# Norms in place on VectorE with four tiles in flight, and a later order of the small products in dilated attention

## Chip, core and metric

The kernel runs on one core of a Trainium2 chip. The engines are TensorE (PE), VectorE (DVE), ScalarE (ACT), GpSimd (POOL) and the queue of SyncE (SP), which issues nearly all transfers. The time is the device time of one execution in microseconds (us); lower is better.

## What is computed

The kernel is one layer of an encoder: x is 1024 positions by 1024 channels in float32. Every sub-layer stands between two RMS norms, and the attention is a mixer of two branches.

```python
h = x + 0.5 * post1(SwiGLU_1(pre1(x)))
h = h + postm(Mixer(prem(h)))
h = h + 0.5 * post2(SwiGLU_2(pre2(h)))

def rms_norm(x, g):
    xf = x.astype(jnp.float32)
    y = xf * lax.rsqrt(jnp.mean(xf * xf, axis=-1, keepdims=True) + EPS)
    return (y * g.astype(jnp.float32)).astype(x.dtype)
...
for pm, ps, pn in parts:          # dilated attention: maximum, denominator, numerator of each pattern
    wgt = jnp.exp(pm - m_all)
    num = wgt * pn if num is None else num + wgt * pn
    den = wgt * ps if den is None else den + wgt * ps
return (num / den).astype(q.dtype)
```

The mixer projects its input once, runs a dense latent attention and the dilated attention (8 heads of 64 channels), projects each by a branch matrix, weighs them by sigmoid gates, adds them, and ends with an output projection.

## The kernel before

The 1024 positions are eight tiles of 128. Every float32 product is made of three products of halves (`xh`, `xl`, `wh`, `wl`: a value rounded, and the rest).

**Who sets the order.** At build time a planner (class `Plan`) runs all parts as processes on a model of the engines. A process asks for an engine with a modelled cost (`act(700, ex)` is a cost of 700 columns), a queue per engine serves the lowest rank first, and `Event` and `Tokens` hold processes back. The order in which the queues are served becomes each engine's instruction order on the chip. So a changed cost, or a `yield 1.0` (a pause in the model), makes no instruction longer; it only moves instructions in the queues. Each engine then works strictly in its order.

**Norms.** `postnorm` takes the result `y` of a sub-layer (in the FFN the accumulator `acc`, filled by L1171; in the mixer `y`, filled by L2560). ACT squares it (L501), POOL makes `rstd` (L309, L311), the gain `y*g` is written to a tile `xn` of its own by POOL for the first 512, 384 or more columns and by DVE for the rest (both L490), and DVE makes `res = xn*rstd + res` (L514). `prenorm` squares `res` (L443), scales it with `rstd` and its gain on DVE (L453), in two of the three places with the last 256 columns by ACT and POOL (L459, L460), and hands the tile to `put`. `put` transposes it on TensorE (L428), ACT casts the result to `xh` (L432) and DVE takes the rest as `xl` (L433). In the second FFN `put` also makes differences of tiles (`xt`, L416). `norm_tok = Tokens(2)` lets two tiles into this chain at a time.

**Dilated attention.** For each head DVE takes the scores from TensorE with their maxima (L2138), ACT takes exponentials (L2149), and two small products with a selection matrix bring the numbers of the patterns together: DVE makes `z` (L2160), TensorE the first product (L2169), a chain of short DVE and ACT steps follows (L2176 to L2205), then `z` again (L2210), the second product (L2217) and `a` (L2228). Then DVE weighs the exponentials (L2246), TensorE transposes them, ACT and DVE split them to `ptd` (L432, L433), and TensorE makes the product with the values. DVE adds its halves to `oT` and `tb` (L2315, L2320), POOL adds the two (L2322), and the result is stored (`ob_d`, L2323). Between these steps TensorE has matmuls of the gate projection (L1495) as filler, and when they are gone those of `branch_a` (L2444). When the last head is stored, `take` loads the heads' results in four pieces (L2378), ACT and POOL split them, and the products of `branch_b` begin; the merge makes `mt` from them (L2521 to L2525) and the output projection follows.

## Time and profile before

| | |
|---|---|
| median of 3 runs | 2434.36 us (2431.82 to 2435.98) |
| profiled execution, device time | 2432.88 us |
| its span in the profile | 2430.7 us |
| TensorE busy | 2294.6 us, 94% of the span |
| VectorE, ScalarE, GpSimd busy | 66%, 43%, 32% |
| granted clock of TensorE, mean | 0.974 of full speed |

The span runs from the first to the last instruction; 2.2 us of the device time lie around it. A busy share is an average over stages: an engine that is busy a third of the whole time may be the one that is waited for in one stage. The granted clock is 1 at 2.4 GHz and 0.5 at 1.2 GHz.

### The profile page before, as it was taken

The numbers are of one execution on the slowest core, as the hardware profiler recorded it, in microseconds if no ns is written. First come the engines' busy times: TensorE is split into PE (matmuls) and PEld (weight loads), VectorE is DVE, ScalarE is ACT, GpSimd is POOL, SyncE is SP. The second block draws the span as 40 slices with busy tenths as digits, with TensorE's granted clock in tenths as the row PEclk, the third lists the DMA queues.
The fourth block names the chain that finished last, engine by engine and source line by source line (L and its number), as shares of the span: only waits on it lengthen the run. The fifth ranks groups of instructions, "written<-read, shape, count | busy, mean of one in ns | idle before, by whom it ended". The sixth has DMA issues, their size and how long they took to land. (4 is left out here: it accounts for less than half of the span.)

```text
span 2430.7 us, 30689 instructions
## 1 busy us (share of the span) xinstructions
PE 2294.6 (94%) x11096; PEld 1920.7 (79%) x11096; DVE 1609.8 (66%) x2669; ACT 1044.0 (43%) x1952; POOL 784.1 (32%) x592
## 2 busy tenths in 40 slices
PE   6999999999979999999998898988979999999997
PEld 4788888788869987888886777776868888887885
DVE  7877878875672105666666766347787778778658
ACT  6233434431153336666655545454433334344111
POOL 2000000354274555756532322575300000006443
PEclk9999999999989999999999999999979999999998
DMA  6234434587352133122223222675533444357762
GB/s 186 83 130 139 173 127 163 195 321 254 134 173 70 62 98 100 38 72 65 61 82 90 79 73 85 194 258 180 182 108 113 163 140 173 116 197 280 259 238 104
DMA packets 197145, 350.17 MB, mean 144 GB/s; under 512 B 32577, under 2 KB 112961, under 8 KB 196481
## 3 DMA queue, kind: packets, MB, share of 16 engines
q1 hardware_dynamic: 196992, 348.21, 42.6%
q8 instruction: 87, 1.43, 0.2%
q14 instruction: 66, 0.53, 0.1%
HBM read 234.78 MB, written 113.38 MB: 143 GB/s over the span
## 5 line engine op out<-in xcount | busy, mean ns | idle before, releaser
L706 PE MATMUL s<-xh,wt 128*128 128x512 f32 x1408 | 453.8, 393 | 10.2 <-DVE uu L807 9.0
L524 POOL TENSOR_TENSOR wdb<-rawd,wdb 128x1024 fp32r<-128x1024 f32 x34 | 87.3, 2567 | 892.4 <-ACT wdb L523 889.3
L706 PE MATMUL b<-xh,wt 128*128 128x512 f32 x1056 | 345.7, 394 | 0.7 <-ACT xh L432 0.6
L706 PEld LDWEIGHTS s<-xh,wt 128*128 128x128 f32 x1408 | 266.2, 189 | 69.8 <-DVE uu L807 10.7
L706 PE MATMUL s<-xl,wt 128*128 128x512 f32 x704 | 275.7, 392 | 0.0
L706 PEld LDWEIGHTS b<-xh,wt 128*128 128x128 f32 x1056 | 200.9, 190 | 44.0 <-ACT xh L432 1.0
L706 PE MATMUL b<-xl,wt 128*128 128x512 f32 x528 | 207.7, 393 | 0.9 <-DVE xl L433 0.9
L1134 PE MATMUL b<-wdb,ha 128*128 128x512 f32 x864 | 202.5, 389 | 0.0
L1134 PE MATMUL s<-wdb,ha 128*128 128x512 f32 x816 | 190.5, 389 | 0.0
L1134 PEld LDWEIGHTS b<-wdb,ha 128*128 128x128 f32 x864 | 162.4, 188 | 33.8
L1134 PEld LDWEIGHTS s<-wdb,ha 128*128 128x128 f32 x816 | 153.1, 188 | 31.8
L1495 PE MATMUL b<-xh,wh 128*128 128x512 f32 x384 | 162.7, 424 | 1.4 <-DVE o L2016 0.8
L1966 POOL TENSOR_TENSOR p<-p,rd 128x1024 f32<-128x1024 f32 x64 | 122.5, 1923 | 117.7 <-DVE rd L1963 112.5
L706 PEld LDWEIGHTS s<-xl,wt 128*128 128x128 f32 x704 | 133.3, 189 | 27.4
L1495 PE MATMUL b<-xl,wh 128*128 128x512 f32 x384 | 153.2, 399 | 0.0
L675 ACT CAST wt<-s 128x512 fp32r<-128x512 f32 x176 | 104.2, 617 | 113.9 <-DVE s L635 59.0
L1495 PE MATMUL b<-xh,wl 128*128 128x512 f32 x384 | 152.9, 398 | 0.0
L524 POOL TENSOR_TENSOR wdb<-td,wdb 128x1024 fp32r<-128x1024 f32 x40 | 108.1, 2706 | 109.7 <-ACT wdb L523 98.6
L428 PE MATMUL b<-cst,p 128*128 128x128 f32 x768 | 107.2, 280 | 22.2 <-DVE ptd L433 14.9
L524 POOL TENSOR_TENSOR wl<-raw,wh 128x512 fp32r<-128x512 f32 (+3 forms) x88 | 110.0, 1267 | 53.5 <-ACT wh L523 46.5
L428 PEld LDWEIGHTS b<-cst,p 128*128 128x128 f32 x768 | 90.1, 143 | 40.0 <-DVE ptd L433 17.5
L676 DVE TENSOR_TENSOR wt<-s,wt 128x512 fp32r<-128x512 f32 x176 | 117.9, 684 | 5.4 <-ACT wt L675 5.1
(298 smaller groups left out, 4989.8 us busy)
## 6 DMA issues: line engine op xcount, KB each, us to landing
hs_d<-hl SPq DMA_DIRECT2D x112, 512.0 KB
ha<-hs_d SPq DMA_DIRECT2D x56, 1024.0 KB
raw<-in_ffn_w_gate_dram SPq DMA_DIRECT2D x48, 512.0 KB
raw<-in_ffn_w_up_dram SPq DMA_DIRECT2D x48, 512.0 KB
rawd<-in_ffn_w_down_dram SPq DMA_DIRECT2D x44, 512.0 KB
raw<-in_w_in_dram SPq DMA_DIRECT2D x28, 512.0 KB
h<-res SPq DMA_DIRECT2D x16, 512.0 KB
lg_d<-lg SPq DMA_DIRECT2D x32, 256.0 KB
```

The source lines that it names most:

```text
L428: T.transpose(b[:rows, i * P : (i + 1) * P], src(i), ident)
L524: yield pool(n, lambda: G.tensor_sub(lo, src, hi))
L675: yield act(512, lambda: A.copy(w[:, 0], src))
L676: yield dve(512, lambda: V.tensor_sub(w[:, 1], src, w[:, 0]))
L706: T.matmul(out(), l, r, start=(first and k == 0 and n == 0), stop=(k == 3 and n == 2), skip_group_check=True,)
L1134: T.matmul(ps, l, r, start=(fresh and n == 0), stop=(n == 5), skip_group_check=True)
L1495: T.matmul(bs.ps, l, r, start=(part == 0 and n == 0), stop=(part == 7 and n == 2))
L1966: yield pool(S, lambda: G.tensor_tensor(bx.p, bx.p, bx.rd.broadcast_to([P, S]), op=ALU.mult))
```

## The change

In the norms the gain is multiplied into `y` itself, all 1024 columns at once and by DVE alone, behind ACT's square; the following `prenorm` writes into the same tile, in two halves on DVE alone, and four tiles are let in. In `put`, two of the four differences are written over the old tile. In the dilated attention the modelled costs of the exponential, of the two steps between the small products and of the weighing are raised, and a pause stands ahead of each small product.

```diff
@@ -105,13 +105,12 @@
     return c
 
 
-PRE1, PREM, PRE2 = 768, 768, D
-POOL1, POOLM, POOL2 = [512] * 8, [384] * 8, [512] * 4 + [1024, 768, 512, 512]
 GATES_FROM = 4
 
 AT_BUFFERS = 7712
 HELD = 4
 EARLY = 4
+NORM = 4
 W0 = 4
 
 
@@ -410,8 +409,8 @@
                     old = [ob[0][:, 0:512], ob[0][:, 512:1024]]
                 for ev in (*scaled, *olds):
                     yield ev
-                tt = [slot([P, 2, 512], name="xt") for _ in range(2)]
-                t1, t2, t3, t4 = tt[0][:, 0, :], tt[0][:, 1, :], tt[1][:, 0, :], tt[1][:, 1, :]
+                tt = slot([P, 2, 512], name="xt")
+                t1, t2, t3, t4 = old[0], tt[:, 0, :], tt[:, 1, :], old[1]
                 for i, o, a_, b_ in ((4, t1, xs[0], old[0]), (5, t2, xs[1], t1), (6, t3, xs[1], xs[0]), (3, t4, old[1], t2)):
                     yield dve(512, lambda: V.tensor_sub(o, a_, b_))
                     spawn(self.block(i, j, o), rank)
@@ -433,7 +432,7 @@
         yield dve(n * P, lambda: V.tensor_sub(lo, box[0], hi))
         plan.release(B1)
 
-    def prenorm(src, g, X, t, rank, split_at, xn=None):
+    def prenorm(src, g, X, t, rank, xn=None):
 
         bx, rs = [], []
 
@@ -446,31 +445,22 @@
         yield act(D + 100, sq)
         yield from rstd_steps(bx[1], D, rs)
         xn = bx[0]
-        m = split_at
-        scaled = [Event(), Event((m > 512) + (m < D))]
-
-        def on_dve(c0, c1, ev):
+        scaled = [Event(), Event()]
+
+        def scale(c0, c1, ev):
             yield dve(c1 - c0, lambda: V.scalar_tensor_tensor(
                 xn[:, c0:c1], src[:, c0:c1], rs[0], g()[:, c0:c1], op0=ALU.mult, op1=ALU.mult,
             ))
             plan.set(ev)
 
-        def on_pool(c0, c1, ev):
-            yield act(c1 - c0, lambda: A.mul(xn[:, c0:c1], src[:, c0:c1], rs[0]))
-            yield pool(c1 - c0, lambda: G.tensor_mul(xn[:, c0:c1], xn[:, c0:c1], g()[:, c0:c1]))
-            plan.set(ev)
-
-        spawn(on_dve(0, 512, scaled[0]), rank)
-        if m > 512:
-            spawn(on_dve(512, m, scaled[1]), rank)
-        if m < D:
-            spawn(on_pool(m, D, scaled[1]), rank)
+        for n in range(2):
+            spawn(scale(512 * n, 512 * n + 512, scaled[n]), rank)
         yield from X.put(t, xn, scaled, rank)
 
     def store(dst, src, kb):
         yield dma(kb, lambda: load(dst, src))
 
-    def postnorm(y, g, res_src, dst, t, box, junk, pool_cols, parts=1):
+    def postnorm(y, g, res_src, dst, t, box, junk, parts=1):
 
         bx, rs = [], []
 
@@ -481,37 +471,26 @@
 
         yield dma(512, ld)
         res = box[0]
-
-        m = pool_cols(t)
-        gained = Event((m > 0) + (m < D))
-
-        def gain_of(cols, eng):
-            def write():
-                eng.tensor_mul(xn[:, cols], y[:, cols], g()[:, cols])
-
-            n = cols.stop - cols.start
-            yield (pool if eng is G else dve)(n, write)
-            plan.set(gained)
-
-        xn = slot([P, D], name="xn")
-        box.append(xn)
+        box.append(y)
+        gained = Event()
 
         def sq():
             ssq = small([P, 1], name="ssq")
             A.activation(junk(), y, AF.Square, accum_out=ssq)
             bx.append(ssq)
 
-        if m:
-            spawn(gain_of(slice(0, m), G), 0)
-        if m < D:
-            spawn(gain_of(slice(m, D), V), 8)
+        def gain_of():
+            yield dve(D, lambda: V.tensor_mul(y, y, g()))
+            plan.set(gained)
+
         yield act(D + 100, sq)
+        spawn(gain_of(), 2)
         yield from rstd_steps(bx[0], D, rs)
         yield gained
         n = D // parts
         for q in range(parts):
             cs = slice(n * q, n * q + n)
-            yield dve(n, lambda: V.scalar_tensor_tensor(res[:, cs], xn[:, cs], rs[0], res[:, cs], op0=ALU.mult, op1=ALU.add))
+            yield dve(n, lambda: V.scalar_tensor_tensor(res[:, cs], y[:, cs], rs[0], res[:, cs], op0=ALU.mult, op1=ALU.add))
             spawn(store(dst[t * P : (t + 1) * P, cs], res[:, cs], 512 // parts), 6)
 
     def raw_tile(w, r0, nk, c0, n):
@@ -1232,7 +1211,7 @@
 
             yield dma(512, ld)
             yield gains0
-            yield from prenorm(bx[0], lambda: gb["g1"], X1, t, 3, PRE1)
+            yield from prenorm(bx[0], lambda: gb["g1"], X1, t, 3)
 
         spawn(one(0), 0)
         yield 0.01
@@ -1245,7 +1224,7 @@
 
     spawn(begin(), 0)
     tail1 = Event()
-    norm_tok = Tokens(2)
+    norm_tok = Tokens(NORM)
 
     def post1(y, t):
         if t == 0:
@@ -1256,8 +1235,8 @@
         yield gains1
         yield norm_tok
         bx = []
-        yield from postnorm(y, lambda: gb["p1"], a["x"], h1, t, bx, lambda: gb["j1"], POOL1.__getitem__)
-        yield from prenorm(bx[0], lambda: gb["gm"], Xm, t, 3, PREM, bx[1])
+        yield from postnorm(y, lambda: gb["p1"], a["x"], h1, t, bx, lambda: gb["j1"])
+        yield from prenorm(bx[0], lambda: gb["gm"], Xm, t, 3, bx[1])
         plan.release(norm_tok)
 
 
@@ -2148,7 +2127,7 @@
                     w = hb.p[i][n // 4][:, n % 4, :]
                     A.activation(w, w, AF.Exp, bias=negm[:, i, n : n + 1], accum_out=md[:, i, 1, n : n + 1])
 
-            yield act(700, ex)
+            yield act(1100, ex)
             plan.set(mev[i])
 
         for i in (1, 0):
@@ -2161,6 +2140,7 @@
             z, md[:, 1].rearrange("p i n -> p (i n)")[:, None, :].broadcast_to([P, 4, 16]),
             mj[:, :, None].broadcast_to([P, 4, 16]), op=ALU.mult,
         ))
+        yield 1.0
         yield B1
         bx = Box()
 
@@ -2192,8 +2172,8 @@
             V.tensor_sub(ee[:, 0, :], md[:, 0, 0, :], mall)
             V.tensor_sub(ju(ee[:, 1, :]), zz[:, :, 0, :], ju(mall))
 
-        yield dve(300, comb)
-        yield act(16, lambda: A.activation(ee, ee, AF.Exp))
+        yield dve(500, comb)
+        yield act(250, lambda: A.activation(ee, ee, AF.Exp))
         wden = small([P, 2, 8], name="wden", bufs=2)
         rd = small([P, 8], name="rdall", bufs=2)
 
@@ -2204,12 +2184,13 @@
             V.reciprocal(rd, rd)
             V.tensor_mul(ee, ee, rd[:, None, :].broadcast_to([P, 2, 8]))
 
-        yield dve(500, comb2)
+        yield dve(900, comb2)
         plan.set(ev[0])
         z2 = small([P, 4, 8], name="z2", bufs=2)
         yield dve(32, lambda: V.tensor_tensor(
             z2, ee[:, 1, None, :].broadcast_to([P, 4, 8]), mm4[:, :, None].broadcast_to([P, 4, 8]), op=ALU.mult,
         ))
+        yield 2.0
         yield B1
 
         def ex2():
@@ -2245,7 +2226,7 @@
                     f = hb.ee[:, 0, n : n + 1] if i == 0 else hb.a23[:, n : n + 1]
                     V.tensor_scalar(w, w, f, None, op0=ALU.mult)
 
-            yield dve2(512 + 100, wgt)
+            yield dve2(512 + 350, wgt)
 
             def block(n):
                 if i == 1:
@@ -2565,8 +2546,8 @@
             yield ev
             yield norm_tok
             bx = []
-            yield from postnorm(y, lambda: gb["pm"], h1, h2, t, bx, lambda: gb["jm"], POOLM.__getitem__)
-            yield from prenorm(bx[0], lambda: gb["g2"], X2, t, 3, PRE2, bx[1])
+            yield from postnorm(y, lambda: gb["pm"], h1, h2, t, bx, lambda: gb["jm"])
+            yield from prenorm(bx[0], lambda: gb["g2"], X2, t, 3, bx[1])
             plan.release(norm_tok)
 
         def outproj():
@@ -2623,7 +2604,7 @@
             gb["j2"] = half_slot([P, D], mybir.dt.bfloat16, name="junk")
             plan.set(gains2)
         yield gains2
-        yield from postnorm(y, lambda: gb["p2"], h2, out, t, [], lambda: gb["j2"], POOL2.__getitem__, 2 if t == NT - 1 else 1)
+        yield from postnorm(y, lambda: gb["p2"], h2, out, t, [], lambda: gb["j2"], 2 if t == NT - 1 else 1)
 
     def second():
         yield out_started
```

TensorE has the same instructions as before, in the same order in both FFNs and in the latent attention. POOL has 38 instructions fewer. The lines of the changed file are some 20 lower: L490 is L483 there, L514 is L493, L453 is L451, L1171 is L1150, L2160 is L2139, L2320 is L2301, L524 is L503.

VectorE where the first FFN ends and the mixer begins, before (each `acc` and `xn` is one tile of 128 positions, `res` its residual, `b` a result of TensorE):

```order
L490 TENSOR_TENSOR xn_5168<-acc_3847,p_738_5058 128x512
L1171 TENSOR_TENSOR acc_3857<-acc_3857,b_5076 128x512
L514 SCALAR_TENSOR_TENSOR res_5132<-xn_5168,rstd_5187,res_5132 128x1024
L1171 TENSOR_TENSOR acc_3870<-acc_3870,b_5085 128x512
L453 SCALAR_TENSOR_TENSOR xn_5144<-res_5122,rstd_5210,gm_5093 128x512
L1171 TENSOR_TENSOR acc_3870<-acc_3870,b_5095 128x512
L453 SCALAR_TENSOR_TENSOR xn_5144<-res_5122,rstd_5210,gm_5093 128x256
L1171 TENSOR_TENSOR acc_3881<-acc_3881,b_5103 128x512
L453 SCALAR_TENSOR_TENSOR xn_5168<-res_5132,rstd_5237,gm_5093 128x512
L1171 TENSOR_TENSOR acc_3881<-acc_3881,b_5113 128x512
L453 SCALAR_TENSOR_TENSOR xn_5168<-res_5132,rstd_5237,gm_5093 128x256
```

And the same stretch now; `acc_3818` to `acc_3850` are the first four tiles:

```order
L483 TENSOR_TENSOR acc_3850<-acc_3850,p_734_5038 128x1024
L1150 TENSOR_TENSOR acc_3870<-acc_3870,b_5114 128x512
L493 SCALAR_TENSOR_TENSOR res_5122<-acc_3837,rstd_5177,res_5122 128x1024
L1150 TENSOR_TENSOR acc_3880<-acc_3880,b_5124 128x512
L1150 TENSOR_TENSOR acc_3880<-acc_3880,b_5136 128x512
L493 SCALAR_TENSOR_TENSOR res_5134<-acc_3850,rstd_5189,res_5134 128x1024
L1150 TENSOR_TENSOR acc_3889<-acc_3889,b_5152 128x512
L1150 TENSOR_TENSOR acc_3889<-acc_3889,b_5167 128x512
L451 SCALAR_TENSOR_TENSOR acc_3818<-res_5102,rstd_5198,gm_5073 128x512 x2
L451 SCALAR_TENSOR_TENSOR acc_3827<-res_5112,rstd_5222,gm_5073 128x512 x2
L451 SCALAR_TENSOR_TENSOR acc_3837<-res_5122,rstd_5229,gm_5073 128x512 x2
L432 TENSOR_TENSOR xl_5235<-b_5237,xh_5233 128x4x128
```

Two tiles were normed and handed on (L453) ahead of the evacuations of the later ones. Now the evacuations of all eight (L1150) come first, and four tiles are scaled one behind the other (L451, two halves each), with no instruction of POOL among them.

VectorE in the third head, before, where `z` for the first small product stands behind `tb`, from which POOL adds `oT`:

```order
L2138 ISA md_11435 128x1
L2320 TENSOR_TENSOR tb_11566<-s_11541,tb_11566 64x1024
L2138 ISA p_1952_11437,md_11435<-b_11582,b_1742_10296 128x256
L2138 ISA md_11435 128x1
L2160 TENSOR_TENSOR z_11597<-md_11435,cst 128x64
L2138 ISA p_1952_11437,md_11435<-b_11575,b_1742_10296 128x256
```

And now:

```order
L2117 ISA md_11384 128x1
L2139 TENSOR_TENSOR z_11580<-md_11384,cst 128x64
L2117 ISA p_1941_11386,md_11384<-b_11560,b_1730_10244 128x256
L2117 ISA md_11384 128x1
L2301 TENSOR_TENSOR tb_11559<-s_11534,tb_11559 64x1024
L2117 ISA p_1941_11386,md_11384<-b_11568,b_1730_10244 128x256
L2117 ISA md_11384 128x1
```

`z` now stands ahead of `tb`. Of the seven heads 2 to 8, `z` stood behind `tb` in all seven; now it stands ahead in heads 3, 5 and 7, and behind in 2, 4, 6 and 8. On TensorE, 9 to 12 filler matmuls and mostly 21 in all stood between the two small products, and now 30 to 39 in most heads; ahead of the first there were 15 to 18 and there are 12 to 21. All in all a head uses about 24 fillers more, so that the gate projection is used up a head earlier.

POOL behind the last head, before (`ro` is a piece of the heads' results, `wl` and `wo` parts of weights):

```order
L2322 TENSOR_TENSOR oT_13500<-oT_13500,tb_13673 64x1024
L524 TENSOR_TENSOR wl_13738<-raw_13713,wh_13737 128x1024
L524 TENSOR_TENSOR xl_13286<-ro_13746,xh_13284 128x1024
L524 TENSOR_TENSOR wl_13782<-raw_13758,wh_13781 128x4x128 x2
L524 TENSOR_TENSOR wl_13820<-raw_13794,wh_13819 128x1024
L524 TENSOR_TENSOR xl_13286<-ro_13807,xh_13284 128x1024
```

And now:

```order
L2303 TENSOR_TENSOR oT_13600<-oT_13600,tb_13781 64x1024
L503 TENSOR_TENSOR wo_13874<-rawo_13865,wo_13874 128x1024
L503 TENSOR_TENSOR wl_13870<-raw_13858,wh_13869 128x4x128 x2
L503 TENSOR_TENSOR xl_12859<-ro_13867,xh_12857 128x1024
L503 TENSOR_TENSOR wo_13885<-rawo_13880,wo_13885 128x1024
L503 TENSOR_TENSOR xl_12859<-ro_13886,xh_12857 128x1024
L503 TENSOR_TENSOR wo_13895<-rawo_13891,wo_13895 128x1024
```

A split of `wo` and one of `wl` now stand between the last `oT` and the first `xl`, and one of `wo` between the first and the second. On TensorE, 117 matmuls of `branch_a` stood between the last head's last product and the first product of `branch_b`; now 57 do. The first twelve matmuls behind these need the first piece, the next the second.

## Rows read from the trace of the kernel before

**Rows 1.** Busy time and granted clock by stretch (columns in the first line)

```profile
core 0: us, PE busy (x) PEld busy (x) DVE busy (x) ACT busy (x) POOL busy (x), PEclk, DMA share, GB/s
...
660.00:760.00 100.00, 82.97 (x487) 75.17 (x487) 70.18 (x83) 44.62 (x91) 63.75 (x70) 0.93 0.39 129
...
1240.00:1545.00 305.00, 269.71 (x1373) 226.01 (x1372) 210.74 (x600) 160.09 (x398) 89.84 (x53) 0.94 0.29 83
...
1590.00:1725.00 135.00, 118.25 (x496) 94.98 (x495) 88.80 (x100) 71.36 (x115) 84.05 (x58) 0.94 0.64 219
...
1750.00:1810.00 60.00, 46.35 (x205) 36.37 (x204) 52.46 (x80) 28.51 (x51) 13.68 (x16) 0.77 0.42 145
...
2390.00:2431.00 41.00, 24.32 (x104) 18.84 (x102) 33.98 (x38) 9.21 (x16) 24.01 (x24) 0.84 0.41 154
```

**Rows 2.** TensorE's waits in the dilated attention: us in total, times, longest

```profile
PE b L428 <- DVE ptd L433: 14.9, 7, 4.4
...
PE b L2169 <- DVE z L2160: 8.5, 4, 3.0
...
PE b L2217 <- DVE z L2210: 4.6, 6, 1.8
...
PE b L428 <- DVE a L2228: 4.0, 2, 2.0
```

**Rows 3.** TensorE's waits from the first FFN to the mixer

```profile
PE b L285 <- DVE xl L433: 6.8, 3, 3.2
...
PE b L285 <- DVE acc L1171: 3.7, 1, 3.7
```

**Rows 4.** VectorE's groups there: count, busy, mean ns, idle before

```profile
L453 DVE SCALAR_TENSOR_TENSOR xn<-res,rstd,gm 128x512 f32<-128x512 f32 (+1 forms) x16 | 20.0, 1281 | 4.5 <-POOL rstd L311 4.5
...
L514 DVE SCALAR_TENSOR_TENSOR res<-xn,rstd,res 128x1024 f32<-128x1024 f32 x8 | 14.8, 1852 | 6.5 <-POOL xn L490 5.1 <-POOL rstd L311 1.4
...
L490 DVE TENSOR_TENSOR xn<-acc,p 128x512 f32<-128x512 f32 x8 | 5.4, 700 | 0.1
```

**Rows 5.** TensorE's waits in merge and output projection

```profile
PE b L428 <- DVE ga L2521: 5.1, 2, 3.7
...
PE b L285 <- DVE ga L2521: 3.4, 1, 3.4
```

**Rows 6.** Timeline of one head's first small product: start, length, engine, line

```profile
1391.35 2.38 POOL L2322 TENSOR_TENSOR oT<-oT,tb 64x1024 f32<-64x1024 f32 x1
...
1393.69 2.47 POOL L524 TENSOR_TENSOR wl<-raw,wh 128x512 fp32r<-128x512 f32 x2
...
1391.69 4.56 DVE L2160 TENSOR_TENSOR z<-md,cst 128x64 f32<-128x64 f32 x1
```

**Rows 7.** Timeline: the norm's VectorE operations beside no GpSimd multiplication

```profile
1690.05 0.75 DVE L453 SCALAR_TENSOR_TENSOR xn<-res,rstd,g 128x512 f32<-128x512 f32 x1 [0.79 <-POOL rstd L311]
...
2403.45 1.28 DVE L514 SCALAR_TENSOR_TENSOR res<-xn,rstd,res 128x1024 f32<-128x1024 f32 x1 [1.50 <-POOL rstd L311]
```

**Rows 8.** Timeline behind the last head's last product

```profile
1543.62 0.51 PE L285 MATMUL s<-ptd,vv 128*128 128x256 f32 x3
...
1549.45 0.58 SPq L2378 DMA_DIRECT2D ro<-ob_d  x1
...
1556.21 2.41 POOL L524 TENSOR_TENSOR xl<-ro,xh 128x1024 fp32r<-128x1024 f32 x1 [4.94 <-ACT xh L523]
...
1563.82 2.40 POOL L524 TENSOR_TENSOR xl<-ro,xh 128x1024 fp32r<-128x1024 f32 x1 [0.33 <-ACT xh L523]
```

**Rows 9.** Timeline: products 128x512 one behind the other

```profile
1742.11 11.04 PE L285 MATMUL b<-wo,mt 128*128 128x512 f32 x48
```

**Rows 10.** VectorE's groups at the end of the program

```profile
L514 DVE SCALAR_TENSOR_TENSOR res<-xn,rstd,res 128x1024 f32<-128x1024 f32 (+1 forms) x9 | 16.0, 1785 | 3.0 <-POOL rstd L311 2.8
...
L1171 DVE TENSOR_TENSOR acc<-acc,b 128x512 f32<-128x512 f32 x16 | 10.6, 677 | 0.1
...
L490 DVE TENSOR_TENSOR xn<-acc,p 128x512 f32<-128x512 f32 (+1 forms) x7 | 5.4, 765 | 0.1
```


## Prediction

> **What bounds the kernel now.** I read the windows first: TensorE's busy time and granted clock, stretch by stretch. In the FFNs and the latent attention TensorE is all but never idle and its order stays as it is, so the change acts only in the stretches of [rows 1]. There the loss of a stretch is its idle time, plus the share of the clock that is missing times its length. From the first FFN to the mixer (660 to 760) that is 100 - 83 = 17.0 us idle and 0.07 x 100 = 7 us of clock, in the dilated attention 35.3 and 18.3, in merge and output projection (1590 to 1725) 16.8 and 8.1, around the second FFN's norm (1750 to 1810) 13.7 and 13.8. In the last stretch TensorE is done early and VectorE, busy for 34.0 of 41 us, sets the end. So a microsecond of idle TensorE comes with about half a microsecond of lost clock (18.3 / 35.3 and 8.1 / 16.8 are both near 0.5; at the mixer 0.4), and I price a removed wait at 1.5 times its length there.
>
> Then I read the waits: which instruction comes last in each stretch. In the dilated attention it is VectorE's `ptd` (14.9 us), the two `z` (8.5 and 4.6) and `a` (4.0) [rows 2]; at the mixer `xl` (6.8) and `acc` (3.7) [rows 3]; in the merge `ga`, twice (5.1 and 3.4) [rows 5]. All of them are VectorE's, and all are short operations. So the third view is the timeline: why is VectorE late? Its `z` of 64 columns takes 4.56 us, from 1391.69 to 1396.25, while GpSimd adds `oT` (2.38) and splits `wl` (2.47), one behind the other, until 1396.16 [rows 6]. VectorE stood still for as long as GpSimd had work. The norm shows the same in its means: `res` of 1024 columns takes 1.28 us when GpSimd has no multiplication and an `L453` of 512 columns 0.75 [rows 7], but in the stretch to the mixer they take 14.8 us for 8 and 20.0 for 16 (half of these are of 256) [rows 4].
>
> The page SBUF — State Buffer of the Trainium skill (section Who interferes with whom) says that a VectorE instruction with two inputs in SBUF and a GpSimd instruction that reads SBUF exclude each other for the whole instruction. This trace agrees: 4.56 us against 2.38 + 2.47.
>
> **First FFN to mixer.** Before, VectorE had 20.0 + 14.8 + 5.4 = 40.2 us of norm here, and 11.0 us of idle time in front of it (6.5 + 4.5) [rows 4]. Now it has 16 halves of 0.75, 8 `res` of 1.28 and 8 gains of 1024, which the trace doesn't show; a gain of 1024 has two inputs like `res`, and I take 1.28 [rows 7]. That is 12.0 + 10.2 + 10.2 = 32.4 us, and the waits for `rstd` (4.5 + 1.4 [rows 4]) stay. VectorE saves 51.2 - 38.3 = 12.9 us. TensorE can get back at most the 10.5 us in which it waited for the norm [rows 3], and not all of it: with four tiles handed on at once it waits in two blocks instead of four. I take half, 5.3, with 0.4 of clock: **-8 us**. Bounds: all 10.5 and its clock, -15; and +4, if a gain of 1024 is as slow as the slow rows (1.85 [rows 4]) and nothing else gets shorter.
>
> **Dilated attention.** With 30 to 39 fillers of 11.04 / 48 = 0.23 us [rows 9] between the two small products, 7 to 9 us, the chain between them is covered; the 4.6 us of the second `z` [rows 2] go. The first `z` was late behind GpSimd's addition, and in heads 3, 5 and 7 it now stands ahead of `tb`, on which that addition waits; I take 5 of the 8.5 us. The waits for `ptd` and `a` I leave: GpSimd still splits weights beside the weighing. 9.6 x 1.5 = **-14 us**. Bounds: with half of `ptd` and `a` gone too, -26; and 0, if each wait only moves to the next step of the same head.
>
> **Behind the last head** the cover is paid for. The last product ends at 1544.1; the first load of the results goes out at 1549.45, and the `xl` of the two pieces end at 1558.6 and 1566.2 [rows 8], 14.5 and 22.1 us behind it. Before, 117 fillers (27 us) hid that. Now 57 fillers last 13.1 us: TensorE waits 1.4 us for the first piece, has 12 products (2.8 us), and waits from 17.3 to 22.1 for the second. That is 6.2 us, with clock **+9 us**. What stands in GpSimd's queue ahead of the first `xl`, a `wo` and a `wl`, fits into the load's time if their weights are there. Bounds: +2, if pieces come as soon as they can (the first load was not waited for before), and +18, if GpSimd's two `wo` (2.4 us each, like the `xl` in [rows 8]) and the stores ahead of the second load in SyncE's queue come on top.
>
> **Merge and output projection.** The `ga` for which TensorE waits, 5.1 + 3.4 us [rows 5], stand behind norm operations that were held by GpSimd's gains. Those gains are gone, and two pairs of products are now made ahead. 8.5 x 1.5 = **-12 us**; bounds -19 (the other waits of the stretch as well) and 0, since four tiles of norm (4 x (1.28 + 1.28 + 1.5) = 16 us by [rows 7]) now stand in one block ahead of a `ga`.
>
> **Second FFN's norm.** The last four tiles no longer wait for one another, but VectorE has all their gains and differences to do in one go and TensorE has fewer fillers left. Going through VectorE's new order with the durations above, the first product that needs all four tiles comes some 2 us earlier relative to the work done, which is less than I can tell: **0 us**, 6 either way. The first norm at the start has 8 x 256 columns more on VectorE (about 3 us by [rows 7]) and 8 short GpSimd steps less: 0, 3 either way.
>
> **End.** VectorE had 16.0 + 10.6 + 5.4 = 32.0 us and waited 3.0 [rows 10]. Now: the same 10.6, 8 gains (10.2), 7 `res` of 1.28 and two halves of 0.75 (10.5): 31.3, and one wait for the last `rstd`, 0.7. **-3 us**; bounds -4 and +3 (gains at 1.85).
>
> The transfers keep their number and size within one instruction, and the exponentials and weighings have their old lengths, since only the planner's costs were raised; what covers them is the same TensorE work.
>
> **Sum:** -8 - 14 + 9 - 12 - 3 = -28 on the profiled execution's 2432.9 us (2430.7 of span and 2.2 around it; the median of the runs shown is 1.5 higher): **2405 us**.
>
> **The rivals.**
> *VectorE becomes the bound (the other side).* The change puts 16,128 columns on it (start 2048, mixer 6144, merge 3072, end 4864): 15.75 x 1.28 = 20 us [rows 7], all in stretches where VectorE is what is waited for. If freeing it from GpSimd gives nothing back, the norms cost 20 us instead of winning 23, and the time is 2432.9 + 20 - 14 + 9 = 2448. It decides from the point where the relief in the norms is under 10 us in all. For it: VectorE is busy for 34 of the last 41 us and GpSimd for 24 [rows 1]. Against it: at the end alone `res` shows 16.0 - 10.5 = 5.5 us of holding and 3.0 of waits [rows 10]. The Trainium skill's page Perfetto Trace Analysis (section Identifying the Most-Contended Engine) says to relieve the engine with the highest occupancy first; here work goes to it, and by that rule this rival would be the outcome.
>
> *The wait moves on.* The heads' chain, not TensorE's order, sets their time; what is no longer waited for at `z` is waited for at `ptd`, which is the largest wait already [rows 2]. The term is 0 instead of -14: 2419. In favour: four heads keep `z` behind `tb`.
>
> *More than I count.* Half of `ptd` and `a` goes too (-26), and all merge waits (-19): 2432.9 - 8 - 26 + 9 - 19 - 3 = 2386.
>
> *No effect.* The gains and the stall behind the last head cancel: 2433.
>
> **How the numbers follow.** Forecast 0.60, VectorE the bound 0.10, the wait moves on 0.17, more than I count 0.08, no effect 0.05. The forecast's own spread, from half of the distance to each term's bounds taken together, is about 2390 to 2422. The 8-in-10 range takes in both middle rivals: 2385 to 2430, leaving VectorE as the bound and no effect outside. 0.2% of 2434 is 4.9 us, about what a measurement of this kernel can tell from no change. Faster by more: the forecast, the moved wait and the larger gain, 0.85 less their slow tails, 0.83. Slower by more: 0.10. Within: 0.07.
>
> **What would show it.** Right: TensorE's waits for the second `z` are gone and those for the first under 4 us; `res` in the norms has a mean near 1.3 us; a new wait of some 5 to 7 us stands behind the last head, before the second half of the first `branch_b` product; between 1590 and 1725 no wait for `ga` over 2 us; in the last stretch VectorE's busy time falls from 34.0 us to about 31 and the waits of `res` for `rstd` from 3.0 to under 1.5. Wrong: `L451` or `L493` wait for `rstd` for more than 10 us in one stretch (GpSimd's small steps held by VectorE's long rows); the waits for `ptd` grow by what `z` lost; or the stall behind the last head is over 12 us, because a `wo` or `wl` whose weights are late holds GpSimd's queue.

## The result and the profile after

The changed kernel takes 2391.85 us (median; 2389.76 to 2394.81) against 2435.17 in the same session: ratio 0.9825, 95% interval 0.9808 to 0.9842. That is 43 us faster where 28 were forecast, inside the range of 2385 to 2430. The time lies 13 us from the forecast of 2405 and 6 us from the rival "more than I count" (2386). The profiled span is 2387.8 us, with a mean granted clock of 0.979.

The windows of the kernel after, cut where its own stages lie (they answer to [rows 1]):

```profile
core 0: us, PE busy (x) PEld busy (x) DVE busy (x) ACT busy (x) POOL busy (x), PEclk, DMA share, GB/s
...
656.00:756.00 100.00, 84.85 (x520) 77.00 (x519) 65.42 (x80) 41.13 (x82) 50.98 (x60) 0.93 0.36 124
1232.00:1524.00 292.00, 277.86 (x1473) 235.83 (x1472) 219.53 (x605) 166.59 (x408) 95.02 (x55) 0.99 0.32 96
1524.00:1562.00 38.00, 28.92 (x113) 21.49 (x111) 5.58 (x5) 18.33 (x25) 28.79 (x15) 0.91 0.86 297
1562.00:1696.00 134.00, 122.89 (x521) 97.62 (x522) 88.33 (x109) 72.31 (x117) 75.28 (x54) 0.95 0.61 210
1696.00:1771.00 75.00, 61.81 (x273) 49.44 (x271) 65.06 (x95) 29.52 (x52) 11.51 (x18) 0.84 0.41 141
2349.00:2388.00 39.00, 24.80 (x110) 20.21 (x108) 33.87 (x42) 9.21 (x16) 11.21 (x16) 0.87 0.27 108
```

In the dilated heads (second row) TensorE is idle for 292.00 - 277.86 = 14.1 us, and the clock takes 0.01 x 292 = 2.9: a loss of 17.1 us, where [rows 1] gave 35.3 + 18.3 = 53.6. Behind the last head (third row) the loss is 9.1 + 3.4 = 12.4, where before only 1.6 was lost. In merge and second norm (fourth and fifth row) it is 17.8 + 25.2 = 43.0, where it was 23.5 + 27.2 = 50.7. Around the first norm (first row) 15.2 us are idle, little less than the 17.0 of before. The rows of before behind the last head, in the merge and in the second norm, cut at the same instructions:

```profile
1543.90:1594.10 50.20, 48.59 (x216) 39.90 (x215) 5.19 (x7) 25.24 (x37) 30.63 (x17) 1.00 0.81 270
1594.10:1733.60 139.50, 124.36 (x523) 100.38 (x524) 93.78 (x108) 72.91 (x117) 84.24 (x59) 0.94 0.61 206
1733.60:1808.60 75.00, 61.35 (x271) 48.84 (x270) 63.51 (x96) 29.14 (x52) 16.42 (x20) 0.82 0.43 146
```

TensorE's waits in the heads (us in total, times, longest), 1232 to 1524, against [rows 2]:

```profile
PE b L427 <- DVE za L2205: 4.2, 5, 1.2
PE b L2198 <- DVE z L2190: 3.9, 1, 3.9
PE b L427 <- DVE ptd L432: 1.8, 5, 0.6
```

The first `z` (now L2139) isn't waited for at all, the second once, in the seventh head, where the order left 12 fillers between the small products. `ptd` fell from 14.9 to 1.8 and `a` from 4.0 to nothing; these two were forecast to stay. But `za`, VectorE's step just ahead of `a`, is new in the list, mostly at the place where `a` was waited for (the ninth of twelve transposes).

Behind the last head, 1524 to 1562, first TensorE's waits and then GpSimd's timeline (start, length):

```profile
PE b L284 <- POOL xl L503: 3.4, 2, 1.9
PE b L284 <- POOL wl L503: 3.3, 2, 2.7
...
PE b L284 <- ACT xh L502: 1.1, 1, 1.1
```

```profile
1531.23 2.40 POOL L503 TENSOR_TENSOR wo<-rawo,wo 128x1024 fp32r<-128x1024 f32 x1 [1.72 <-ACT wo L502]
...
1538.84 2.35 POOL L503 TENSOR_TENSOR xl<-ro,xh 128x1024 fp32r<-128x1024 f32 x1 [2.72 <-ACT xh L502]
1541.15 2.37 POOL L503 TENSOR_TENSOR wo<-rawo,wo 128x1024 fp32r<-128x1024 f32 x1
1545.17 2.37 POOL L503 TENSOR_TENSOR xl<-ro,xh 128x1024 fp32r<-128x1024 f32 x1 [1.65 <-ACT xh L502]
```

The two `xl` end 16.7 and 23.0 us behind the last product of the heads (1524.5), near the 14.5 and 22.1 of the forecast. A `wl` behind them is late as well.

In merge and output projection, 1562 to 1696 (against [rows 5]):

```profile
PE b L284 <- ACT mt L2505: 7.6, 3, 6.0
...
PE b L284 <- DVE ga L2502: 0.8, 1, 0.8
```

`ga` is gone from the waits, but `mt` has come in its place. ScalarE's timeline shows why: its cast stands behind two casts of `wo`, ahead of which ScalarE was idle for 5.33 and 3.64 us, for the load of their weights. The cast's input was ready at 1595.6, when VectorE's L2504 ended.

```profile
1598.38 1.05 ACT L502 CAST wo<-rawo 128x1024 fp32r<-128x1024 f32 x1 [5.33 <-DMA rawo<-in_w_out_dram]
1603.06 1.04 ACT L502 CAST wo<-rawo 128x1024 fp32r<-128x1024 f32 x1 [3.64 <-DMA rawo<-in_w_out_dram]
1604.02 0.61 ACT L2505 CAST mt<-ga 128x512 fp32r<-128x512 f32 x1
```

At the mixer, 656 to 756 (against [rows 3]), four tiles handed on in one block are waited for:

```profile
PE b L427 <- DVE xl L432: 7.6, 3, 5.0
PE b L427 <- DVE acc L451: 7.6, 4, 2.2
```

VectorE's groups there (count, busy, mean ns, idle before; against [rows 4]), and then those of the end, 2349 to 2388 (against [rows 10]):

```profile
L451 DVE SCALAR_TENSOR_TENSOR acc<-res,rstd,gm 128x512 f32<-128x512 f32 x16 | 15.0, 985 | 1.8 <-POOL rstd L310 1.8
L483 DVE TENSOR_TENSOR acc<-acc,p 128x1024 f32<-128x1024 f32 x8 | 12.1, 1524 | 0.0
...
L493 DVE SCALAR_TENSOR_TENSOR res<-acc,rstd,res 128x1024 f32<-128x1024 f32 x8 | 10.1, 1277 | 0.8 <-POOL rstd L310 0.7
```

```profile
L1150 DVE TENSOR_TENSOR acc<-acc,b 128x512 f32<-128x512 f32 x16 | 10.7, 682 | 1.1 <-PE b L284 1.0
L493 DVE SCALAR_TENSOR_TENSOR res<-acc,rstd,res 128x1024 f32<-128x1024 f32 (+1 forms) x9 | 10.1, 1158 | 0.1
L483 DVE TENSOR_TENSOR acc<-acc,p 128x1024 f32<-128x1024 f32 x8 | 9.7, 1218 | 0.0
```

`res` takes 1.28 us as forecast, and no longer waits for `rstd` at the end.

### The profile page after: what moved, and what is told of

Read it like the earlier page. It is cut to its first block, busy times and chain, and to the rows that moved or that the text cites. A ratio compares the mean times of both kernels' runs of the same rounds, so it can differ in the third digit from the quotient of the medians.

```text
span 2387.8 us, 30581 instructions
## 1 busy us (share of the span) xinstructions
PE 2277.5 (95%) x11096; PEld 1907.8 (80%) x11096; DVE 1608.5 (67%) x2670; ACT 1038.3 (43%) x1936; POOL 736.9 (31%) x552
## 5 line engine op out<-in xcount | busy, mean ns | idle before, releaser
L503 POOL TENSOR_TENSOR wdb<-rawd,wdb 128x1024 fp32r<-128x1024 f32 x34 | 87.0, 2559 | 903.8 <-ACT wdb L502 900.8
L1474 PE MATMUL b<-xh,wh 128*128 128x512 f32 x384 | 157.8, 411 | 1.2 <-DVE ct L432 0.6
L503 POOL TENSOR_TENSOR wdb<-td,wdb 128x1024 fp32r<-128x1024 f32 x40 | 104.3, 2608 | 107.8 <-ACT wdb L502 90.4
L503 POOL TENSOR_TENSOR wl<-raw,wh 128x512 fp32r<-128x512 f32 (+3 forms) x88 | 107.7, 1239 | 45.2 <-ACT wh L502 44.4
L685 PEld LDWEIGHTS b<-xl,wt 128*128 128x128 f32 x528 | 100.2, 190 | 22.1 <-DVE xl L432 1.5
```

The lines of the kernel that those rows point to most:

```text
L503: yield pool(n, lambda: G.tensor_sub(lo, src, hi))
L685: T.matmul(out(), l, r, start=(first and k == 0 and n == 0), stop=(k == 3 and n == 2), skip_group_check=True,)
L1474: T.matmul(bs.ps, l, r, start=(part == 0 and n == 0), stop=(part == 7 and n == 2))
```

## The experiments

Every number below is of a program with the whole computation; only orders, tiles and engines differ. The table holds the loss of TensorE in us (idle time, and missing clock times length, from each kernel's windows) in stretches cut at the same instructions: heads = first small product to last product with the values; behind = from there to the first product of the output projection; merge and norm = from there to one fixed product in the second FFN. For the first norm, where the clock's two digits alone are worth 2 us, it holds by how much the way from the first down product of the first FFN to the first small product became shorter or longer than before. (In the heads the digits are worth 1.5 us.) The last column counts, in the program's order, the filler matmuls in the eight heads, and those of them that stand between the two small products. (675 against 576 is 12 more a head, not the 24 that the part on the change names.) The runs of before next to each kernel have medians of 2432 to 2435; so differences between kernels are taken from the ratios, times 2434.

| kernel | median us | ratio, interval | first norm | heads | behind | merge and norm | fillers |
|---|---|---|---|---|---|---|---|
| before | 2435.17 |  | 0 | 53.6 | 1.6 | 50.7 | 576, 168 |
| after | 2391.85 | 0.9825 [0.9808, 0.9842] | -3.0 | 17.1 | 12.4 | 43.0 | 675, 249 |
| e1 norms only | 2419.57 | 0.9949 [0.9935, 0.9963] | -2.8 | 56.3 | 0.6 | 42.1 | 576, 168 |
| e2 dilated only | 2411.54 | 0.9910 [0.9897, 0.9924] | +2.9 | 17.2 | 13.5 | 52.2 | 675, 249 |
| e3 exponential's cost old | 2385.89 | 0.9808 [0.9793, 0.9823] | -2.6 | 28.4 | 0.0 | 42.9 | 573, 273 |
| e9 weighing's cost old | 2382.38 | 0.9788 [0.9775, 0.9802] | -1.0 | 15.2 | 0.8 | 41.1 | 566, 270 |
| e10 no pauses | 2392.30 | 0.9832 [0.9819, 0.9846] | -2.8 | 27.8 | 0.9 | 38.4 | 575, 224 |
| e11 pauses only | 2397.61 | 0.9844 [0.9831, 0.9858] | -1.5 | 28.1 | 1.7 | 41.2 | 633, 258 |
| e12 chain's costs old | 2402.19 | 0.9869 [0.9855, 0.9882] | -2.2 | 35.2 | 2.6 | 48.6 | 615, 225 |
| e6 before, gains on VectorE | 2413.07 | 0.9916 [0.9901, 0.9931] | -11.1 | 52.7 | 1.4 | 46.3 | 576, 168 |
| e7 after, gains shared | 2408.92 | 0.9903 [0.9887, 0.9920] | +5.1 | 15.9 | 13.4 | 51.3 | 675, 249 |
| e4 two tiles | 2399.35 | 0.9862 [0.9846, 0.9877] | -12.7 | 17.0 | 12.4 | 62.8 | 675, 249 |
| e5 two tiles at the mixer | 2381.63 | 0.9793 [0.9779, 0.9808] | -9.8 | 19.8 | 12.8 | 41.9 | 675, 249 |
| e8 e5, weighing's cost old | 2373.00 | 0.9757 [0.9742, 0.9771] | -13.0 | 14.1 | 1.6 | 47.5 | 566, 270 |

Kernels in which 12 instead of 3 fillers stand ahead of the first small product (after, e2, e4, e5, e7, e8, e9, e12) carry 9 x 0.23 = 2.1 us of moved work in the first-norm column, by [rows 9]; e3, e10 and e11, with 6, carry 0.7.

The losses are those of one profiled execution of each kernel, the times are medians. That execution took 4.6 us more than the median in e3 and in e5, 2.6 more in e8 and 7.3 less in e11 (2390.27 against 2397.61), in the others at most 2.3 more or less; so the losses of e3, e5, e8 and e11 explain their medians only so far.

**The two halves.** e1 is the kernel after with the old numbers of the dilated attention, e2 the kernel before with the new ones (all seven lines of the diff in that function).

> The norms as changed, the dilated attention's planner numbers as before; TensorE's order in the heads is then the old one. If the two parts are independent (theory one), the heads keep their 53 us of loss and there is no stall behind the last head: the gain is what the after-trace shows outside (start 3, first norm 3, merge and second FFN's norm about 10, end 4, some 4 in between), about 2411 to 2417. If the norms also feed the heads' gain, by freed tiles or transfers that start earlier (rival), the heads lose clearly less than 53 us here and the time is under 2405.

> The norms as before, the dilated attention's numbers as changed. Theory one (cover): the heads' loss falls from 53 us to about 17 as in the after-trace, the stall behind the last head costs 12: about 2408 to 2413. Rival (VectorE freed by the norms' change is what helps): loss in the heads over 35 us, about 2425.

The norms alone give 13.5 us, the new order alone 21.5; e1's time lies 2.6 us over the range that was expected, e2's inside its range. e1's waits in the heads are those of [rows 2] almost to the digit, so freeing VectorE elsewhere did nothing for the heads:

```profile
PE b L427 <- DVE ptd L432: 14.4, 7, 4.0
PE b L2148 <- DVE z L2139: 8.5, 4, 3.0
```

e2 has the heads of the kernel after (17.2) and its stall (13.5). In its merge the old waits for `ga` still stand, beside the new one for `mt` (and one of 6.9 us for `y`):

```profile
PE b L285 <- ACT mt L2526: 9.7, 3, 5.9
...
PE b L285 <- DVE ga L2523: 4.5, 3, 3.4
```

By the ratios the halves would give 12.4 + 21.9 = 34 us together, and the kernel after gains 43. The three intervals together are worth some 6 us, and the difference lies in no one stretch; whether the halves help each other stays open.

**One number at a time.** Each of these is the kernel after with part of the new numbers taken back.

```diff
-            yield act(1100, ex)
+            yield act(700, ex)
```

> The whole change, but the exponential's modelled cost back at 700. TensorE's order then has 30 to 39 fillers between the small products in all eight heads and about four times 57 fillers left behind the last one. Theory (cover is what counts, and the later heads pay for it): heads as good as in the changed kernel, no stall behind the last head, 2378 to 2384. Rival (the exponential's cost is what puts the first z ahead of GpSimd's addition and so removes its wait): waits for the first z of 5 us and more come back with their clock, 2388 to 2396.

```profile
1235.00:1513.00 278.00, 260.72 (x1372) 219.86 (x1371) 214.46 (x606) 159.76 (x399) 90.40 (x53) 0.96 0.33 91
1513.00:1561.00 48.00, 48.00 (x213) 39.73 (x213) 6.24 (x7) 24.65 (x35) 29.16 (x17) 1.00 0.82 276
```

The heads lose 11 us more than in the kernel after, 3.2 in idle time and the rest in clock, and behind the last head nothing is lost: 165 fillers are left there instead of 57. (The expectations say 213 or so and 105, with the 48 products of `branch_b` that stand among them.) With 573 used in the heads against 675 the sum is the same within a few: one stock, and what the heads use is missing behind them. Neither theory came out whole: the heads are not as good as in the kernel after, but no first `z` is waited for; TensorE waits for `ptd` (5.0 us, and 2.5 ahead of the product with the values) and `za` (5.0). By the ratios it is 4 us faster than the kernel after, just inside what the two intervals allow for no difference.

```diff
-            yield dve2(512 + 350, wgt)
+            yield dve2(512 + 100, wgt)
```

> The kernel after with the weighing's modelled cost back at 512+100 columns, the other raised costs and both pauses kept, four tiles in flight. 21 to 36 fillers stand between the small products as in the kernel after, but only 9 instead of 12 among the transposes, and 214 instead of 105 are left behind the last head. Theory A (a fixed stock of fillers, which the heads and the place behind the last head share): the dilated heads lose about as little as in the kernel after (17.1 us), because what covers them stands between the small products, and the 12.4 us behind the last head go; with the mixer's first norm as in the kernel after the time is about 2383 us, 8 to 10 under the kernel after and 8 to 10 over the run that has this cost and two tiles in the first norm. Rival B (the fillers among the transposes are what removed the waits for ptd): with 9 there, ptd comes back to 10 us or more with its clock, and the time is 2390 to 2398 us.

```profile
1235.00:1503.00 268.00, 255.49 (x1363) 217.36 (x1362) 208.89 (x605) 158.25 (x397) 88.47 (x53) 0.99 0.33 93
1503.00:1553.00 50.00, 49.49 (x220) 40.41 (x218) 5.18 (x7) 25.52 (x36) 32.57 (x18) 1.00 0.84 274
```

Theory A holds: 9.0 us under the kernel after by the ratios. The heads lose no more with 566 fillers instead of 675, `ptd` is at 3.6 us in all, and the stall is gone; the largest wait is now one for the scores' maxima `md`, 6.0 us in eight times. The raised cost of the weighing bought nothing and took the cover behind the last head. Rival B falls. The comparison with the kernel before says more: that one has 576 fillers in its heads and loses 53.6 us, this one has 566 and loses 15.2. What differs on TensorE is the place: 270 instead of 168 between the small products, 9 instead of 6 among the transposes behind them, and, in exchange, in the third head 3 instead of 12 between the score products and the second transposes. VectorE's order differs as well: in heads 2 to 8 of e9 no first `z` is held (0.20 to 0.22 us each, where before the mean was 2.31). How much of the 38 us belongs to either no run separates.

```diff
-        yield 1.0
...
-        yield 2.0
```

> The kernel after without the two pauses ahead of the small products, all raised costs kept. 24 to 36 fillers stand between the small products still, 9 to 15 among the transposes in place of 12, 211 are left behind the last head in place of 105. Theory A (what counts is the number of fillers in each gap, not which number of the planner puts them there): the heads lose between 17 and 28 us, with waits for ptd in the heads with 6 fillers among the transposes, and behind the last head nothing; 2385 to 2391 us. Rival B (the pauses are what covers the chain): the heads lose 40 us or more, 2400 us or more.

e11 is the reverse: both pauses stay, and the four costs go back.

> The kernel after with the two pauses and with the old costs of the exponential, the chain and the weighing. The fillers are spread as unevenly as 6 to 24 ahead of the first small product, 24 to 39 between the two, 9 to 15 among the transposes; 153 are left behind the last head. Theory A (number of fillers in each gap): waits for the first z in the four heads with 6 to 9 fillers ahead of it, nothing behind the last head; the heads lose about 25 us, and the time is near the kernel after's, 2387 to 2394 us. Rival B (the raised costs are what covers the chain): the heads lose 40 us or more, 2400 us or more.

```diff
-        yield dve(500, comb)
-        yield act(250, lambda: A.activation(ee, ee, AF.Exp))
+        yield dve(300, comb)
+        yield act(16, lambda: A.activation(ee, ee, AF.Exp))
...
-        yield dve(900, comb2)
+        yield dve(500, comb2)
```

> The kernel after with the two steps between the small products at their old modelled costs; the exponential, the weighing and the pauses as in the kernel after. 24 to 33 fillers stand between the small products, 3 to 6 fewer than in the kernel after in most heads, 12 among the transposes, and 165 instead of 105 are left behind the last head. Theory A (24 fillers, 5.5 us, are enough for the chain): the heads lose 17 to 22 us and the stall behind the last head is gone, 2380 to 2386 us. Rival B (the chain needs the 30 to 39 that the kernel after gives it): the second z is waited for again, 1 us or more in most heads, and the gain behind the last head is lost there: 2390 us or more.

Without the pauses the heads lose 27.8 us, with the pauses alone 28.1: either alone gives some 70% of the heads' gain. That is about A's loss in both, but not its waits: without the pauses TensorE waits for the first `z` (5.2 us, four times) and for `za` (8.9 and 2.1), more than for `ptd` (3.9), and with them alone for `za` (8.3), `ptd` (5.3) and the second `z` (4.9, three times), not the first. The times lie above A's ranges, by 1.3 us in e10 and 3.6 in e11. In e12 A falls: the heads lose 35.2 us, with waits

```profile
PE b L427 <- DVE za L2205: 9.9, 4, 3.9
PE b L2198 <- DVE z L2190: 4.8, 2, 2.5
```

The two waits for the second `z` stand in the sixth and the eighth head, which have 24 fillers between the products; so 24 don't always cover the chain, but "most heads" of B was wrong too. 5.6 us more are lost than in the kernel after in merge and norm, where `mt` is waited for 12.9 us. Its casts stand there behind a cast of `wo` and a gate `ga` for whose loads ScalarE was idle for 5.1 and 4.0 us; why these loads come later I did not settle.

**The norms.** e6 is the kernel before with one thing changed: the gains and the last 256 columns go to VectorE. Tiles in flight (two), the tile `xn` and the dilated attention stay.

```diff
-PRE1, PREM, PRE2 = 768, 768, D
-POOL1, POOLM, POOL2 = [512] * 8, [384] * 8, [512] * 4 + [1024, 768, 512, 512]
+PRE1, PREM, PRE2 = D, D, D
+POOL1, POOLM, POOL2 = [0] * 8, [0] * 8, [0] * 8
```

> The kernel before, with all gains on VectorE and nothing else (own tile for the result, two tiles in flight, old heads). The prediction's reason for the norms (VectorE is freed from GpSimd's long multiplications): res falls to a mean near 1.3 us, and the time falls by most of what the norms gave (13 us): 2420 to 2426. Rival (VectorE as the bound, its added 20 us count): 2436 to 2450. Rival (the order, four in flight, is what counts): 2430 to 2436.

e7 is the kernel after with the gains shared between GpSimd and VectorE as before, still in place and with four tiles.

> The whole change, but behind ACT's square the gain of the post-norms is split as before between GpSimd (the first 512 or 384 columns, up to 1024 at the end) and VectorE, still in place and with four in flight; the pre-norm stays on VectorE. If the freed VectorE is what gives the norms' gain, res goes back to a mean over 1.6 us and 6 to 12 us are lost against the changed kernel: 2398 to 2404. If only the order counts, 2390 to 2394.

VectorE's groups at the mixer in e6, and then in e7:

```profile
L514 DVE SCALAR_TENSOR_TENSOR res<-xn,rstd,res 128x1024 f32<-128x1024 f32 x8 | 14.8, 1858 | 0.2 <-POOL rstd L311 0.2
L453 DVE SCALAR_TENSOR_TENSOR xn<-res,rstd,gm 128x512 f32<-128x512 f32 x16 | 14.6, 941 | 2.5 <-POOL rstd L311 2.5
L490 DVE TENSOR_TENSOR xn<-acc,p 128x1024 f32<-128x1024 f32 x8 | 10.8, 1354 | 0.1
```

```profile
L452 DVE SCALAR_TENSOR_TENSOR acc<-res,rstd,gm 128x512 f32<-128x512 f32 x16 | 19.8, 1264 | 1.9 <-POOL rstd L311 1.9
L499 DVE SCALAR_TENSOR_TENSOR res<-acc,rstd,res 128x1024 f32<-128x1024 f32 x8 | 12.0, 1499 | 4.3 <-POOL rstd L311 4.0
```

With the gains on VectorE, e6 has 16 halves in 14.6 us, where [rows 4] show 20.0 for fewer columns, and all but no wait ahead of `res`. It is 19 us faster than the kernel before (median of its runs 2432.41), with more columns on VectorE; its time lies 7 us under the range that was expected. One sign failed: at the mixer `res` keeps its mean (1858 ns against 1852). Five of the eight take 1.28 us; three took 2.2 to 3.4 beside GpSimd's splits of weights (`wc`, `wl`), which the change leaves on GpSimd; in e4, e5 and e8 three take 2.8 to 3.3 in the same way. With the gains shared again e7 has 19.8 us for the same 16 halves that take 15.0 in the kernel after, waits 4.0 for `rstd` ahead of `res`, and is 19 us slower than the kernel after by the ratios, where 6 to 12 were expected (some 8 at the first norm, 8 in merge and norm, 4 from there to the end). Both say that GpSimd's gains held VectorE up. By the ratios e6 is also 8 us faster than e1 (some 5 of interval), which has all of the norms' change: what that adds, four tiles and the gain in place, cost 8 us at the first norm and won 4 in merge and norm.

```diff
-NORM = 4
+NORM = 2
```

> The whole change with two tiles in flight instead of four. If four in flight is what made the first norm gain only 3 of the predicted 8 us (TensorE waits once per block of four), the stretch to the mixer gets 3 to 5 us shorter here, while merge and second FFN's norm may lose as much: 2388 to 2393. If four in flight is what gives the norms' gain, 2398 or more.

```diff
-    norm_tok = Tokens(NORM)
+    norm_tok, mix_tok = Tokens(2), Tokens(NORM)
...
-            yield norm_tok
+            yield mix_tok
```

> The whole change, with two tiles in flight in the norm between first FFN and mixer and four in the one between mixer and second FFN. By stretch, two tiles in flight everywhere lost 12 us from the first FFN to the latent attention where four lost 28, but 15 us more in the merge and 5 more at the second FFN's norm. Theory: the two places are independent; the loss is 12 at the first place and 18 at the second: 9 us (what the landmark at the first small product showed) below the changed kernel, 2381 to 2385. Rival: the lower loss at the first place is paid back in the heads or the merge, 2390 to 2394.

The window of 100 us around the first norm in e5, to be read beside the kernel after's 84.85 busy at 0.93:

```profile
653.00:753.00 100.00, 92.67 (x555) 85.29 (x555) 70.88 (x88) 43.43 (x88) 49.01 (x58) 0.97 0.39 125
```

Two tiles are better at the mixer by 7 to 10 us (first norm -12.7 and -9.8 against -3.0), four are better in the merge: there e4 loses 62.8 - 43.0 = 20 us more, with waits for `ga` back at 6.2 us and one of 5.6 for `y`. e5 takes each where it is good and is 7.8 us under the kernel after by the ratios.

**The version that beats both.** e8 joins e5 and e9: two tiles at the mixer, four in the merge, the weighing at its old cost.

> As the first kernel of this call, and the modelled cost of the weighing back at 512 + 100. TensorE's order then has 30 to 36 fillers between the small products in all eight heads, 9 instead of 12 among the transposes, and no stall behind the last head since twice as many fillers are left. Theory (fillers are a stock that is spent once): heads lose 17 to 28 us, nothing behind the last head, 2375 to 2381. Rival (the weighing's cost is what removed the waits for ptd): the waits for ptd come back with 8 us and more, 2384 or more.

```profile
1224.00:1491.00 267.00, 252.87 (x1362) 214.71 (x1362) 209.04 (x605) 157.83 (x395) 88.53 (x53) 1.00 0.33 93
1491.00:1541.00 50.00, 49.24 (x218) 40.16 (x216) 5.18 (x7) 24.71 (x35) 31.75 (x18) 1.00 0.84 269
```

2373.00 us (2372.59 to 2375.60), 0.9757 of the kernel before. The two edits add up within the intervals (some 5 us on each difference): by the ratios two tiles give 7.8 us with the new weighing cost and 7.5 with the old, the old cost 9.0 with four tiles and 8.8 with two. The time is 2 us under the theory's range, and the heads lose 14.1 where 17 to 28 were expected.

## Why the prediction came out as it did

The sign and the range were right. The sum was right within 15 us only because terms missed in opposite directions, which was luck: the dilated attention gained 22.5 us more than forecast, outside its bounds, and three other terms came out 11 us worse. (Three products of the working are off by its own figures: 5.3 us with 0.4 of clock are 7.4 and not 8, 8.5 x 1.5 is 12.8 and not 12, and half of `ptd` and `a` on top of 14 gives 28.6 and not 26. The first two cancel in the sum.)

- **Dilated attention, -14 forecast, -36.5 measured** (53.6 to 17.1), outside its bounds. The step that failed is "The waits for `ptd` and `a` I leave: GpSimd still splits weights beside the weighing." GpSimd does, and VectorE's `ptd` is as long as it was (40.8 us before, 40.5 after), and so is the first of its two weighings (36.4 and 36.3); the second fell from 25.1 to 19.7.

  Yet `ptd` and `a`, 18.9 us of waits, are down to 1.8 of `ptd` and 4.2 of `za`, and in e9, where the second weighing takes 24.0 and the first 31.7, to 3.6 and 2.6. So these waits were not made by GpSimd's hold alone; VectorE was late with the chain, the weighing and `ptd` one after the other, and fillers that stood behind these steps now stand ahead of them. All seven waits for `ptd` in [rows 2] stood at one place, ahead of the last four transposes of a head's first weighing, behind three fillers (six in the first head); now nine stand there in six heads (6 x 0.23 = 1.4 us more), and the waits left there are 0.3 to 0.6 us. In two heads at least a late first `z` didn't make them: in heads 4 and 6 TensorE didn't wait for it, waited 0.3 and 0.5 us for the second `z`, and then still 2.0 for `a` and 2.1 for `ptd`.

  e9 shows most plainly what the new order does, with no more fillers in the heads than the kernel before and less than a third of its loss. That `z` was held is right as far as it goes, but in the kernel after the hold largely moved on, to short operations for which TensorE doesn't wait at once. Of the second `z` 3.9 of 4.6 us stayed, in one head. VectorE's groups in the heads, of the kernel before (1240 to 1545) and after (1232 to 1524):

```profile
L2160 DVE TENSOR_TENSOR z<-md,cst 128x64 f32<-128x64 f32 x7 | 16.2, 2308 | 0.0
L2144 DVE TENSOR_SCALAR negd<-md 128x2 f32<-128x2 f32 x56 | 13.6, 270 | 0.0
```

```profile
L2123 DVE TENSOR_SCALAR negd<-md 128x2 f32<-128x2 f32 x56 | 31.6, 595 | 0.0
...
L2139 DVE TENSOR_TENSOR z<-md,cst 128x64 f32<-128x64 f32 x7 | 4.9, 705 | 0.0
```

- **Behind the last head, +9 forecast, +10.8 measured.** The mechanism and the place are right (two `xl`, 16.7 and 23.0 us behind the last product). The waits for the two pieces are 4.5 us (`xl` 3.4, `xh` 1.1) where 6.2 were forecast; a late `wl` came on top, 3.3 us, and an `mt`, 1.2. e3 and e9 confirm that it is the missing fillers: with 165 left the stall is gone.
- **First FFN to mixer, -8 forecast, -3.0 measured** (-5.1 with the 2.1 us of moved fillers). VectorE's part was right: 37.2 us and 2.6 of waits, 39.8, against 38.3 forecast and 51.2 before; halves were longer than 0.75 and gains longer than 1.28, waits shorter. The step "I take half" failed: the blocks of four tiles cost TensorE 15.2 us of waits in place of 10.5. e4 and e5, with two tiles, have -12.7 and -9.8 there, and e6, with two tiles, shows that the relief from GpSimd is worth -11.1 by itself.
- **Merge and second norm, -12 and 0 forecast, -7.7 measured** (50.7 to 43.0). The waits for `ga` went as forecast. The step left out is ScalarE's queue: `mt` waits there behind casts of `wo`, whose loads are late.
- **End, -3 forecast, -5.1 measured** from the fixed product in the second FFN to the end. VectorE's three groups take 30.5 us (31.3 forecast) and wait 0.1 for `rstd` (0.7).
- **Start, 0 forecast, -3.0 measured** to the first down product; the bound was 3.
- **VectorE becomes the bound** fell with e6, which moves the columns to VectorE alone, with two tiles, and gains 19 us. VectorE's busy time didn't even grow with the 16,128 columns, since the operations beside them got shorter; the pages of before and of e6 (busy us, share of the span, instructions):

```profile
PE 2294.6 (94%) x11096; PEld 1920.7 (79%) x11096; DVE 1609.8 (66%) x2669; ACT 1044.0 (43%) x1952; POOL 784.1 (32%) x592
```

```profile
PE 2290.8 (95%) x11096; PEld 1920.9 (80%) x11096; DVE 1600.0 (66%) x2670; ACT 1038.9 (43%) x1936; POOL 733.2 (30%) x552
```

The Trainium skill, page Perfetto Trace Analysis, section Identifying the Most-Contended Engine, says to optimize the engine with the highest occupancy first. The prediction took that to speak against the change. These runs don't decide against the page: over the whole kernel that engine is TensorE (94%, its weight loads 79%), VectorE leads only in single stretches such as the last of [rows 1], and in e6 its busy time fell by 9.8 us.
- **The other rivals.** "The wait moves on" fell: `ptd` shrank. "No effect" fell. Of "more than I count" the first half, `ptd` and `a`, came true and more, even with the 4.2 us of `za`; the second, all of the merge's waits, didn't.

Of the signs, `res` near 1.3 us, the first `z` under 4 us, `ga` under 2 us and the waits for `rstd` at the end came as written. The second `z` is not gone (3.9 us, once). The stall behind the last head, forecast at 5 to 7 us of waits, has 9.1; with its clock, 12.4, it is just over the 12 that were named as a sign of being wrong, and a `wl` was late, as that sign says, but behind the two `xl`. VectorE's busy time in the last stretch didn't fall to 31: it is 33.87 of 39 us, since a window of that length holds other work too (42 instructions against 38).

## What to carry to other kernels

An engine at 66% can be made faster by more work, if that work was done by an engine that held it up, since its busy time holds the time in which it stands still: compare an operation's mean length beside the other engine and apart from it before sharing work out. Filler work that hides waits is a stock: its place in a stage can matter more than its number, and what a stage spends without need is missing behind it, so take back every raised cost that buys no cover. Set the tiles in flight for each place apart, since one number can be best in one norm and worst in the next.

## What the hardware showed that was not expected

A microsecond of idle TensorE was not always worth half a microsecond of clock. Before, 35.3 us of idle time in the heads came with a granted clock of 0.94; the 14.1 us left in the kernel after came with 0.99, and 14.1 us in e8, where no wait was longer than 2.0 us, with 1.00, that is at the level of 2.4 GHz all the time. e3, with 17.3 us of idle time and no wait over 2.7 us in its heads, had 0.96 again, and e10, with 25.0 us and none over 2.6, 0.99. So a factor of 1.5 is no constant; which waits make the clock fall no run here separates, and executions of one kernel differ too (e11: a mean of 0.974 to 0.979 over the whole).

A short VectorE operation with one input was held as well: `negd` of two columns, 0.27 us in the mean before and 0.60 after. In the heads of the kernel after 36 of the 56 take 0.16 us in the mean. The other 20 take 0.7 to 2.4; each ran beside GpSimd throughout and ended within 0.03 us of the end of a GpSimd operation, as here (start, length):

```profile
1457.27 2.20 DVE L2123 TENSOR_SCALAR negd<-md 128x2 f32<-128x2 f32 x1
1457.05 2.41 POOL L503 TENSOR_TENSOR xl<-ro,xh 128x1024 fp32r<-128x1024 f32 x1 [2.32 <-ACT xh L502]
```

Six of the short ones lay beside GpSimd too, for over 0.1 us, so not every meeting holds. The Trainium skill, page SBUF — State Buffer, section Who interferes with whom, lists `tensor_scalar`, under conditions on its operands, among the operations that can take the pair of ports shared with GpSimd. The 20 ends in this trace agree with it.
